# Block products in sevens: two more pairs of strips per layer in a two-layer decoder trunk

## The chip, the cores and the metric

The kernel runs on one core of one Trainium2 chip. The metric is the time of one execution on the device in microseconds (us), as the median of several runs; lower is better. Per core there are a matrix engine (PE in the profile, TensorE), a vector engine (DVE), a scalar engine (ACT), GpSimd (POOL) and the queue that issues most loads (SP). The engines run side by side and wait for one another through semaphores; each takes its own instructions in a fixed order.

## The reference, cut to what matters

A trunk of two layers over 256 tokens with 2048 features. Each layer is attention, then a gated feed-forward part with a short convolution, then a gate with an embedding; everything is residual, in float32.

```python
for i in range(DEPTH):                       # DEPTH = 2
    h = rms_norm(x, attn_norm_w[i])
    x = x + mixer_a(h, ...)                  # layer 0; mixer_b(...) over shared keys and values in layer 1
    x = x + conv_ffn(rms_norm(x, ffn_norm_w[i]), ffn_w_up[i], ffn_conv_w[i], ffn_conv_b[i], ffn_w_down[i])
    gate = jax.nn.sigmoid(rms_norm(x, ple_norm_w[i]) @ ple_w_gate[i])
    x = x + gate * (p[i] @ ple_w_proj[i])

def conv_ffn(h, w_up, conv_w, conv_b, w_down):   # h @ w_up: 256 x 2048 by 2048 x 11264
    u = causal_depthwise_conv(h @ w_up, conv_w, conv_b)
    gate, val = u[..., :D_FF], u[..., D_FF:]     # D_FF = 5632
    return (jax.nn.silu(gate) * val) @ w_down    # 256 x 5632 by 5632 x 2048
```

The attention parts end in an output projection (`wo_a`, 2048 x 2048; `wo_b`, 1536 x 2048), whose result is added to `x` and normed: that is the input `h` of the up projection.

## The kernel before

**Words.** A *block* is 128 input features; an activation block (`h`, `g`, `o`) holds them for all 256 tokens, as a high and a low part, which together carry float32. A *strip* is 512 output columns of a weight matrix; its result is two PSUM banks, one for each 128 tokens (*token half*). For one block, one strip and one token half `add_block` (L339) issues three matmuls of 128x512: L342 (low activation, high weights), L343 (high, low) and L344 (high, high). A *tile* is two blocks of weights of one strip, so 12 matmuls.

**Weights.** `weights` (L277) loads four blocks of a strip at once (`raw`, 1 MB, SP queue, L288; four such buffers). ACT makes the high part of a tile (`whi`, L305) and DVE the low part (`wlo`, L306). The pool `wsp` has four pairs of `whi`/`wlo` (`NWSP`, L70): a pair is free again when PE has read it. So in the steady state ACT and DVE work three to four tiles ahead of PE, and wait for PE to free a pair.

**Seven for eight.** `Seven` (L437) takes four blocks of two strips. Two token halves, two pairs of blocks and two strips would be eight products of two blocks (six matmuls each). It makes seven: `block_sums` (L413) adds and subtracts quarters of the activations once (DVE L423 to L428, split by ACT L431 and DVE L432); `load` (L476) brings both strips' four blocks; `first` to `seventh` each split one weight combination (`parts`, L460, ACT L464 and DVE L465) and multiply (L474), and DVE adds weights in between (L458). `fourth` ends with four additions on PSUM (L514 to L517), which prepare the four result banks. `first` to `fourth` are put among the tiles of the strip before (the *host* strip), at the places in `HEADS`, and `fifth` to `seventh` among those of the pair's own first strip, at `TAILS`; the pair then goes on from its fifth block. The weight combinations are written over the loaded `raw` tiles, which stay taken until the seventh product.

**Where sevens are.** Of 11 pairs of up strips (gate and value) per layer, five go in sevens; of the down projection, which comes in two parts (blocks 0 to 19 after five pairs of up strips, blocks 20 to 43 after the other six), strips 2 and 3 of each part.

**The order around the change.** `add_strips` (L903) makes a projection whose result is added to `x` (L917, DVE), squared for the norm (L211, ACT), and turned from tokens to features: DVE transposes (L243), POOL sends the result to DRAM and fetches it back (L246, L254), and `split_x` (L143 ACT, L144 DVE) makes four blocks `h` of it. The turned strip is used one strip later (`Turned.add`); the last strip's four blocks come late, by `products` (L359), which begins the next matrix with the blocks that are there. For `wo_b` three strips (0, 1, 2) are begun with eight blocks and then get their last four, and strip 3 follows with all twelve; for `wo_a` two strips are begun so.

**The scheduler.** The program's text is not the order on the engines: a scheduler places instructions by priority and its own estimate of times; the weight splits have a higher priority (`AHEAD`) than the `block_sums`.

Of the kernel before, what the change touches and what calls it, by code (L numbers as in the profile page):

```python
# [50 lines left out]
HEADS, TAILS = {8: (1, 3, 5, 7), 6: (1, 2, 4, 5)}, (0, 1, 3)  # L51
# [24 lines left out]
def tile_trunk(ctx, tc, head_d, xT_d, x_d, pT_d, pos_d, vec_d, cst_d, csb_d, wqkv, wo_a, wkv, wq_b, wo_b, wup, wdn, wpg, wpp, gfin_d, out_d):  # L76
# [244 lines left out]
    def strip_v(W, s, xs, base=0, tail=2, ringed=0, begun=None, ends=True, before=lambda k0: None, room=None, halved=False, ready=None, hooks={}):  # L321
# [8 lines left out]
        for k, o, hi, lo in (g for group in it for g in group):  # L330
            if ps[o] is None:
                ps[o] = bank("accv", "acc") if room is None else room[:, o]
                if halved and o:
                    ps[o] = ps[o][:, :S]
            c = slice((o - 1) * S, o * S) if halved and o else slice(0, 512)
            add_block(ps[o], xs[k], min(o, 1), hi[:, c], lo[:, c], k == 0 and not begun, ends and k == n - 1)
# [22 lines left out]
    def products(jobs, xs, late=None, at=0, then={}, side=2, seven=None):  # L359
# [7 lines left out]
        if late is not None:  # L367
            n = len(xs)

# [4 lines left out]
            def before(k0):  # L374
                if k0 == at:
# [4 lines left out]
            hooks = {}  # L380
            if seven is not None:
                tiles = n // 2
                hooks = {tiles - 4: seven.load, tiles - 2: seven.first, tiles - 1: seven.second}
            begun = [
                strip_v(
                    W,
                    s,
                    xs[:n],
                    base,
                    ends=False,  # L390
                    before=before if i == side - 1 else lambda k0: None,
                    room=two_banks() if i == 2 else None,
                    hooks=hooks if i == side - 1 else {},
                )
                for i, (W, s, base) in enumerate(jobs[:side])
            ]
# [5 lines left out]
            hooks = [{0: seven.third}, {0: seven.fourth}] if seven is not None else [{}] * side  # L402
            for b, (W, s, base), more in zip(begun, jobs, hooks):
                yield strip_v(W, s, xs[n:], base + n, begun=b, ready=ready, hooks=more)
                ready = None
            jobs = jobs[side:]
        if seven is not None:
            yield from seven.both()
            jobs = []
        for W, s, base in jobs:  # L410
            yield strip_v(W, s, xs, base)
# [25 lines left out]
    class Seven:  # L437
# [4 lines left out]
        def __init__(self, W, s0, s1, xs, sums, base=0, two=True):  # L442
            self.W, self.strips, self.base, self.two = W, (s0, s1), base, two
# [5 lines left out]
        def value_bank(self, o):  # L449
            if not self.two:  # L450
                return bank("values", "acc")
            if o == 0:
                self.banks = two_banks()
            return self.banks[:, o]
# [29 lines left out]
        def first(self):  # L484
            self.c11 = bank("gates")
# [10 lines left out]
        def second(self):  # L496
            self.c12 = self.value_bank(0)
# [6 lines left out]
        def third(self):  # L504
            self.c21 = bank("gates", "acc")
            self.product(self.c21, self.sums[1], self.parts(self.u), True)

        def fourth(self):
            self.c22 = self.value_bank(1)
# [20 lines left out]

        def go_on(self):
            hooks = dict(zip(TAILS, (self.fifth, self.sixth, self.seventh)))
            yield strip_among(self.W, self.strips[0], self.xs, hooks, [self.c11, self.c21], 4, self.base)

        def end(self, hooks):
            return strip_among(self.W, self.strips[1], self.xs, hooks, [self.c12, self.c22], 4, self.base)

        def both(self):
            yield from self.go_on()
            yield self.end({})  # L540
# [173 lines left out]
    def mixer_a(xs, rc, first):  # L714
# [4 lines left out]

        def turned(which, g, ps=None):  # L720
            us = scaled(ps or strip_v(wqkv, 4 * which + g, xs), (rq, rc)[which], ring_room)
# [500 lines left out]
```

## Time and profile before

| what | value |
|---|---|
| three runs | 2280.32, 2280.76, 2280.83 us; median 2280.76 us |
| the profiled execution: its own time, its span | 2284.18 us, 2282.4 us |
| mean granted PE clock | 0.998 |
| busy: PE, DVE, ACT, POOL | 2267.6, 1686.4, 1318.8, 327.7 us |
| moved by DMA | 538.44 MB, 236 GB/s |

Busy time of PE counts overlapping matmuls once; each matmul's row lasts longer than the distance to the next start. A row "A ... <-B" in the lists reads: result, inputs, count, busy time, mean of one in ns, and the idle time before it with what ended it.

### The profile page before, as it was taken

To read this page: it belongs to the slowest core of one execution; us is meant where nothing else is said; L and a number is where in the kernel's file an instruction comes from. 1 tells how busy PE (TensorE), PEld (TensorE's weight loads), DVE (VectorE), ACT (ScalarE), POOL (GpSimd) and SP (SyncE) were. 2 spreads that over 40 slices of the span, in tenths; PEclk is the share of its full clock that TensorE was granted. 3 is DMA by queue.
4 is the path that set the end of the run, shared out by engine and by line. 5 is a ranking of instruction groups with operands and counts; after the bars stand their busy time and mean duration, and the time that the engine had idled before them with its cause. 6 is when DMAs were issued, how large, how long until landed. Compare 5 with 4: busy or idle time off the path is not lost.

```text
span 2282.4 us, 28059 instructions
## 1 busy us (share of the span) xinstructions
PE 2267.6 (99%) x10113; PEld 1878.2 (82%) x10113; DVE 1686.4 (74%) x2471; ACT 1318.8 (58%) x1766; POOL 327.7 (14%) x575
## 2 busy tenths in 40 slices
PE   9999999999999999999999999999999999999998
PEld 7888888888888888888888888888888888888887
DVE  7656667688875888876667665768887588887665
ACT  6554555666644666655565554666664466665554
POOL 0211111111100111101111331211110011110100
PEclk9999999999999999999999999999999999999999
DMA  8777767676755767758676786767675576775863
GB/s 307 251 240 240 237 224 254 216 271 230 252 199 196 262 232 242 264 185 272 207 266 236 254 261 225 259 217 266 228 252 202 195 256 234 238 265 187 273 222 120
DMA packets 98348, 538.44 MB, mean 236 GB/s; under 512 B 16672, under 2 KB 17568, under 8 KB 46752
## 3 DMA queue, kind: packets, MB, share of 16 engines
q1 hardware_dynamic: 63360, 435.46, 54.6%
q0 software_dynamic: 32560, 95.98, 13.8%
q10 hardware_dynamic: 2288, 5.21, 0.6%
q8 instruction: 79, 1.29, 0.2%
q14 instruction: 61, 0.50, 0.1%
HBM read 486.52 MB, written 50.07 MB: 235 GB/s over the span
## 4 chain that ended last, share of the span: by engine, by line
PE 97%; DMA 2%; ACT 0%; POOL 0%; DVE 0%; issue 0%; POOLq 0%
PE accv L343 22%; PE accv L342 22%; PE accv L344 22%; PE two L343 4%; PE two L344 4%; PE two L342 4%; PE gates L343 4%; PE gates L344 4%; PE gates L342 4%; PE gates L474 3%; PE two L474 3%; PE two L583 1%; DMA turned<-there 1%; DMA there<-y 1%; PE keys L583 0%; POOL turned L254 0%
## 5 line engine op out<-in xcount | busy, mean ns | idle before, releaser
L306 DVE TENSOR_TENSOR wlo<-raw,whi 128x1024 fp32r<-128x1024 f32 (+1 forms) x768 | 931.5, 1215 | 455.2 <-ACT whi L305 452.7
L305 ACT ACTIVATE whi<-raw 128x1024 fp32r<-128x1024 f32 (+1 forms) x768 | 807.6, 1053 | 699.0 <-PE accv L344 426.1
L342 PE MATMUL accv<-whi,h 128*128 128x512 f32 (+1 forms) x1688 | 655.2, 388 | 2.4 <-DVE h L144 2.4
L344 PE MATMUL accv<-whi,h 128*128 128x512 f32 (+1 forms) x1688 | 656.3, 389 | 0.0
L343 PE MATMUL accv<-wlo,h 128*128 128x512 f32 (+1 forms) x1688 | 655.6, 388 | 0.0
L342 PEld LDWEIGHTS accv<-whi,h 128*128 128x128 f32 x1688 | 316.9, 188 | 68.6 <-DVE h L144 1.9
L343 PEld LDWEIGHTS accv<-wlo,h 128*128 128x128 f32 x1688 | 317.0, 188 | 65.8 <-DVE wlo L306 0.7
L344 PEld LDWEIGHTS accv<-whi,h 128*128 128x128 f32 x1688 | 317.0, 188 | 64.6
L246 POOL DMA_DIRECT2D there<-y x162 | 91.5, 565 | 1249.4 <-DVE y L243 1229.9
L254 POOL DMA_DIRECT2D turned<-there x324 | 189.5, 592 | 471.8 <-DMA there<-y 208.7
L464 ACT ACTIVATE whi<-raw 128x1024 fp32r<-128x1024 f32 x98 | 103.7, 1058 | 80.8 <-PE accv L344 68.2
L465 DVE TENSOR_TENSOR wlo<-raw,whi 128x1024 fp32r<-128x1024 f32 x98 | 119.8, 1222 | 34.8 <-ACT whi L464 34.5
L342 PE MATMUL accv<-whi,g 128*128 128x512 f32 x352 | 136.9, 389 | 0.0
L343 PE MATMUL accv<-wlo,g 128*128 128x512 f32 x352 | 136.9, 389 | 0.0
L344 PE MATMUL accv<-whi,g 128*128 128x512 f32 x352 | 136.9, 389 | 0.0
L342 PE MATMUL gates<-whi,h 128*128 128x512 f32 x240 | 93.4, 389 | 0.0
L343 PE MATMUL gates<-wlo,h 128*128 128x512 f32 x240 | 93.4, 389 | 0.0
L344 PE MATMUL gates<-whi,h 128*128 128x512 f32 x240 | 93.4, 389 | 0.0
L342 PE MATMUL two<-whi,h 128*128 128x512 f32 x240 | 93.4, 389 | 0.0
L343 PE MATMUL two<-wlo,h 128*128 128x512 f32 x240 | 93.4, 389 | 0.0
L344 PE MATMUL two<-whi,h 128*128 128x512 f32 x240 | 93.4, 389 | 0.0
L243 DVE STREAM_TRANSPOSE y<-u 128x512 f32<-128x512 f32 x122 | 84.1, 700 | 1.8 <-DMA there<-y 1.3
(224 smaller groups left out, 3024.2 us busy)
## 6 DMA issues: line engine op xcount, KB each, us to landing
raw<-in_wup SPq DMA_DIRECT2D x176, 1024.0 KB, 5.6
raw<-in_wdn SPq DMA_DIRECT2D x88, 1024.0 KB, 5.3
there<-y POOLq DMA_DIRECT2D x171, 256.0 KB, 5.2
turned<-there POOLq DMA_DIRECT2D x324, 128.0 KB, 5.1
raw<-in_wqkv SPq DMA_DIRECT2D x40, 1024.0 KB, 6.6
raw<-in_wpg SPq DMA_DIRECT2D x32, 1024.0 KB, 5.0
raw<-in_wkv SPq DMA_DIRECT2D x24, 1024.0 KB, 5.2
raw<-in_wo_a SPq DMA_DIRECT2D x16, 1024.0 KB, 5.4
```

The costliest lines, as they stand in the source:

```text
L243: last["turned"] = nc.vector.transpose(y.rearrange("p (b o r) -> p o b r", b=4, o=4), strip.rearrange("p (o b c) -> p o b c", o=4, b=4)).ins
L246: nc.gpsimd.dma_start(there[t * P : (t + 1) * P], y)
L254: nc.gpsimd.dma_start(z[32 * b : 32 * b + 32].rearrange("p a o r -> p a (o r)"), back[b])
L305: last["high"] = nc.scalar.activation(hi[:, c], r, AF.Copy).ins
L306: last["low weights"] = nc.vector.tensor_tensor(lo[:, c], r, f32(hi[:, c]), op=OP.subtract).ins
L342: nc.tensor.matmul(ps, xl, hi, start=first, stop=False, skip_group_check=again)
L343: nc.tensor.matmul(ps, xh, lo, start=False, stop=False, skip_group_check=again)
L344: nc.tensor.matmul(ps, xh, hi, start=False, stop=final, skip_group_check=again)
L464: last["high"] = nc.scalar.activation(hi, r, AF.Copy).ins
L465: last["low weights"] = nc.vector.tensor_tensor(lo, r, f32(hi), op=OP.subtract).ins
L474: nc.tensor.matmul(ps, x, y, start=begins, stop=ends, skip_group_check=True)
L583: run.append(nc.tensor.matmul(*args, skip_group_check=True, **kw).ins)
```

## The change

Four sevens more: in each layer the first pair of up strips (gate strip 0, value strip 11), hosted by strip 3 of the output projection (`wo_a`, `wo_b`), and strips 0 and 1 of the second part of the down projection, hosted by the last up strip. `Seven` gets its banks by a list of tags (`take`); `products` begins a pair from a `Seven` that already has four blocks (`first`, `skip = 4`), with `fifth` to `seventh` among the tiles of its first strip; `end` can host the next seven among its six tiles. The sums of blocks 0 to 3 are made once, earlier than before, and shared (`began.sums`, `first.sums`). Parts of the diff under `if False` build nothing and are left out.

```diff
-HEADS, TAILS = {8: (1, 3, 5, 7), 6: (1, 2, 4, 5)}, (0, 1, 3)
+HEADS, TAILS = {10: (2, 4, 6, 8), 8: (1, 3, 5, 7), 6: (1, 2, 4, 5)}, (0, 1, 3)
+PLAN = {-4: "load", -2: "first", -1: "second"}, {0: "third"}, {0: "fourth"}
...
@@ products
+            skip = 4 if first else 0
...
+            if first:
+                hooks[0] = first.rest()
+                begun[:2] = first.banks()
+            if seven:
+                hooks[side - 1].update({(n - skip) // 2 + i: getattr(seven, f) for i, f in plan[0].items()})
+                later = [{i: getattr(seven, f) for i, f in p.items()} for p in plan[1:]]
+            for i, (W, s, base) in enumerate(jobs[:side]):
+                begun[i] = strip_v(
                     W,
                     s,
-                    xs[:n],
-                    base,
+                    xs[skip:n],
+                    base + skip,
                     ends=False,
+                    begun=begun[i],
...
-        for W, s, base in jobs:
-            yield strip_v(W, s, xs, base)
+        for i, (W, s, base) in enumerate(jobs):
+            after = host() if i == len(jobs) - 1 else None
+            yield strip_v(W, s, xs, base, hooks=after.begin(len(xs) // 2) if after else {})
@@ class Seven
+        def rest(self):
+            return dict(zip(TAILS, (self.fifth, self.sixth, self.seventh)))
+
+        def banks(self):
+            return [self.c11, self.c21], [self.c12, self.c22]
...
+        def end(self, after=None):
+            hooks = after.begin(len(self.xs) // 2 - 2) if after else {}
+            return strip_among(self.W, self.strips[1], self.xs, hooks, self.banks()[1], 4, self.base)
@@ ffn
-            sums = block_sums(xs)
+            sums = began.sums if began and late is not None else block_sums(xs)
...
+                    if final and hosts:
+                        after = down[0] = Seven(wdn[i], 0, 1, gs, block_sums(gs[:4]), 4 * strips[0], ("att", "acc", "acc", "acc"))
...
-                        yield from products([(W, s, 0), (W, v, 0)], xs, late, None)
+                        yield from products([(W, s, 0), (W, v, 0)], xs, late, None, first=began)
...
-                        yield from now.go_on()
-                        yield now.end(after.begin(6) if after else {})
+                        yield now.go_on()
+                        yield now.end(after)
...
+            if first:
+                seven = Seven(wdn[i], 2, 3, gs, first.sums, base, ("acc", "two", "acc", "two"))
@@ main loop
-        h, late = add_strips(wo_a if i == 0 else wo_b, o, G_FFN + i * KB, norm, late=o_late, at=(8, 4)[i], side=2 + i)
+        host = lambda h: Seven(wup[i], 0, FB // 4, h, block_sums(h[:4]), 0, ("att", "acc", "acc", "acc"))
+        h, late, began = add_strips(
...
-        h, late, norm = ffn(i, h, late, rc)
+        h, late, norm = ffn(i, h, late, rc, began)
```

**The order on the engines.** In all PE has 24 matmuls fewer (9930 rows for 9954), ACT 20 rows more (12 `whi`, 8 copies), DVE 44 more (12 `wlo`, 16 additions of weights, 16 on PSUM); POOL and SP have as many as before. Line numbers of the changed file are three to ten higher: L308 there is L305 here, L345 to L347 are L342 to L344, L474 is L464, L484 is L474, L146 is L143, L441 is L431, L161 is L158. Numbers behind a name only tell buffers apart.

First place, second layer, ACT, from the fifth tile of strip 3 of `wo_b` on; before (`whi_2272` and `whi_2274` are the fifth and sixth tile, `whi_2301` is the first tile of the up projection):

```order
L305 ACTIVATE whi_2272_12039<-raw_2271_12037 128x1024
L143 ACTIVATE h_2236_11879<-turned_2228_11834,vec_75 128x256
L143 ACTIVATE h_2237_11882<-turned_2228_11834,vec_75 128x256
L143 ACTIVATE h_2238_11885<-turned_2228_11834,vec_75 128x256
L143 ACTIVATE h_2239_11888<-turned_2228_11834,vec_75 128x256
L305 ACTIVATE whi_2274_12055<-raw_2271_12037 128x1024
L158 ACT_TABLE_LOAD
L305 ACTIVATE whi_2301_12146<-raw_2300_12144 128x1024
L305 ACTIVATE whi_2305_12164<-raw_2300_12144 128x1024
```

and in the changed kernel (`whi_2306` and `whi_2311` are the fifth and sixth tile of strip 3, `whi_2309` is the fourth product's weights, `whi_2329` the fifth product's, `sum_2275` and `sum_2279` the two halves of the sums, `h_2265` to `h_2268` the turned strip 1):

```order
L308 ACTIVATE whi_2306_12140<-raw_2305_12138 128x1024
L474 ACTIVATE whi_2309_12157<-raw_2281_12025 128x1024
L146 ACTIVATE h_2265_11977<-turned_2257_11932,vec_75 128x256
L146 ACTIVATE h_2266_11980<-turned_2257_11932,vec_75 128x256
L146 ACTIVATE h_2267_11983<-turned_2257_11932,vec_75 128x256
L146 ACTIVATE h_2268_11986<-turned_2257_11932,vec_75 128x256
L308 ACTIVATE whi_2311_12172<-raw_2305_12138 128x1024
L161 ACT_TABLE_LOAD
L441 ACTIVATE sum_2275_12009<-u_2274_12002 128x512
L474 ACTIVATE whi_2329_12237<-raw_2281_12025 128x1024
L441 ACTIVATE sum_2279_12021<-u_2278_12014 128x512
L308 ACTIVATE whi_2332_12249<-raw_2331_12247 128x1024
```

The turned strips are split later relative to the tiles, and the two sums now stand on ACT between the last tile of strip 3 and the first ones of the up projection.

PE at the end of strip 3 there; before, the up projection's first tile follows at once:

```order
L343 MATMUL accv_2263_11980<-wlo_2275_12056,o_2215_11754 128x512
L344 MATMUL accv_2263_11980<-whi_2274_12055,o_2215_11754 128x512
L342 MATMUL accv_2303_12150<-whi_2301_12146,h_2236_11879 128x512
L343 MATMUL accv_2303_12150<-wlo_2302_12147,h_2236_11879 128x512
L344 MATMUL accv_2303_12150<-whi_2301_12146,h_2236_11879 128x512
```

and in the changed kernel (`seven_2288`, `2294`, `2302` and `2308` are the result banks c11, c12, c21 and c22; weights 2295, 2303, 2309 and 2329 are those of the second, third, fourth and fifth product):

```order
L347 MATMUL accv_2287_12042<-whi_2311_12172,o_2229_11788 128x512
L484 MATMUL seven_2288_12049<-whi_2329_12237,h_2252_11919 128x512
L484 MATMUL seven_2294_12080<-whi_2295_12081,sum_2276_12010 128x512
L484 MATMUL seven_2294_12080<-wlo_2296_12082,sum_2275_12009 128x512
L484 MATMUL seven_2294_12080<-whi_2295_12081,sum_2275_12009 128x512
L484 MATMUL seven_2302_12127<-whi_2303_12128,sum_2276_12010 128x512
L484 MATMUL seven_2302_12127<-wlo_2304_12129,sum_2275_12009 128x512
L484 MATMUL seven_2302_12127<-whi_2303_12128,sum_2275_12009 128x512
L484 MATMUL seven_2308_12156<-whi_2309_12157,sum_2276_12010 128x512
L484 MATMUL seven_2308_12156<-wlo_2310_12158,sum_2275_12009 128x512
L484 MATMUL seven_2308_12156<-whi_2309_12157,sum_2275_12009 128x512
L484 MATMUL seven_2288_12049<-wlo_2330_12238,h_2252_11919 128x512
```

The second, third and fourth product, which the text puts among strip 3's tiles, stand behind its last tile, since their sums come late there.

Second place, first layer, PE, in the fourth tile (2996) of strip 3 of `wo_a`, in the changed kernel (before, only the rows on `accv` stand there); `sum_537` and `sum_541` are the low halves of the two sums:

```order
L484 MATMUL seven_558_2983<-whi_559_2984,sum_537_2895 128x512
L484 MATMUL seven_558_2983<-wlo_560_2985,sum_536_2894 128x512
L484 MATMUL seven_558_2983<-whi_559_2984,sum_536_2894 128x512
L346 MATMUL accv_548_2927<-wlo_562_2997,o_292_1587 128x512
L347 MATMUL accv_548_2927<-whi_561_2996,o_292_1587 128x512
L345 MATMUL accv_548_2927<-whi_561_2996,o_293_1590 128x512
L346 MATMUL accv_548_2927<-wlo_562_2997,o_293_1590 128x512
L484 MATMUL seven_558_2983<-whi_559_2984,sum_541_2907 128x512
```

Here the second product runs inside strip 3, one tile later than an evenly placed one would.

More of the change, by code (lines that the diff above doesn't have):

```diff
@@ L319, in steps, with strip_v @@
             yield [(k0 + i, o, hi[i], lo[i]) for k0, hi, lo in held for i in range(2)]
-    def strip_v(W, s, xs, base=0, tail=2, ringed=0, begun=None, ends=True, before=lambda k0: None, room=None, halved=False, ready=None, hooks={}):
+    def strip_v(W, s, xs, base=0, tail=2, ringed=0, begun=None, ends=True, before=lambda k0: None, room=None, halved=False, ready=None, hooks={}, again=False):
         n = len(xs)
@@ L335, in strip_v @@
             c = slice((o - 1) * S, o * S) if halved and o else slice(0, 512)
-            add_block(ps[o], xs[k], min(o, 1), hi[:, c], lo[:, c], k == 0 and not begun, ends and k == n - 1)
+            add_block(ps[o], xs[k], min(o, 1), hi[:, c], lo[:, c], k == 0 and not begun, ends and k == n - 1, again)
         return ps
@@ L357, in two_strips, with products @@
         return out
-    def products(jobs, xs, late=None, at=0, then={}, side=2, seven=None):
+    def products(jobs, xs, late=None, at=0, then={}, side=2, first=None, seven=None, plan=PLAN, host=lambda: None):
         jobs = list(jobs)
@@ L401, in products @@
                 add()
-            hooks = [{0: seven.third}, {0: seven.fourth}] if seven is not None else [{}] * side
-            for b, (W, s, base), more in zip(begun, jobs, hooks):
-                yield strip_v(W, s, xs[n:], base + n, begun=b, ready=ready, hooks=more)
+            for b, (W, s, base), more in zip(begun, jobs, later):
+                yield strip_v(W, s, xs[n:], base + n, begun=b, ready=ready, hooks=more, again=bool(first))
                 ready = None
             jobs = jobs[side:]
-        if seven is not None:
-            yield from seven.both()
-            jobs = []
-        for W, s, base in jobs:
-            yield strip_v(W, s, xs, base)
+        if seven:
+            yield seven.go_on()
+            yield seven.end(host())
+            return
+        for i, (W, s, base) in enumerate(jobs):
+            after = host() if i == len(jobs) - 1 else None
+            yield strip_v(W, s, xs, base, hooks=after.begin(len(xs) // 2) if after else {})
     def block_sums(xs):
@@ L718, in mixer_a @@
         q, k, ws, os = {}, {}, {}, []
+        sums = block_sums(xs[:4]) if False else None
+        pair = [None]
         def turned(which, g, ps=None):
+            if ps is None and pair[0]:
+                ps = pair[0].end() if which else pair[0].go_on()
             us = scaled(ps or strip_v(wqkv, 4 * which + g, xs), (rq, rc)[which], ring_room)
@@ L901, in mixer_b, with add_strips @@
         return os, lambda: use(z)
-    def add_strips(W, xs, gain_of, norm, base=0, late=None, at=6, side=2):
+    def add_strips(W, xs, gain_of, norm, base=0, late=None, at=6, side=2, first=None, seven=None, plan=PLAN, host=None):
         out = []
@@ L911, in add_strips, with hosted @@
         turned = Turned(use)
-        seven = Seven(W, 2, 3, xs, block_sums(xs[:4]), base) if gain_of is None or base else None
-        for s, ps in enumerate(products([(W, s, base) for s in range(4)], xs, late, at, side=side, seven=seven)):
+        begun = [None]
+        def hosted():
+            if host is not None:
+                begun[0] = host(out)
+            return begun[0]
+        jobs = [(W, s, base) for s in range(4)]
+        for s, ps in enumerate(products(jobs, xs, late, at, {}, side, first, seven, plan, hosted)):
             if norm is not None and s == 3:
@@ L1051, in ple @@
                 gf.append(t)
-        gates = products([(wpg[i], s, 0) for s in range(3 if gain_of is None else 4)], xs, late, None)
+        seven = None
+        if False and gain_of is not None:
+            seven = Seven(wpg[i], 2, 3, xs, block_sums(xs[:4]), 0, ("att", "acc", "acc", "acc"))
+        jobs = [(wpg[i], s, 0) for s in range(3 if gain_of is None else 4)]
+        gates = products(jobs, xs, late, None, seven=seven, plan=PLAN_GATE)
         for s in range(4):
```

96 lines of the change are left out of this document (55 added, 41 removed).

## The prediction

> **What bounds the kernel now.** I read the busy shares and the chain of the page first, then the list of PE's waits, then windows over single stretches. The page's rows:
>
> ```profile
> PE 2267.6 (99%) x10113; PEld 1878.2 (82%) x10113; DVE 1686.4 (74%) x2471; ACT 1318.8 (58%) x1766; POOL 327.7 (14%) x575
> ...
> PE 97%; DMA 2%; ACT 0%; POOL 0%; DVE 0%; issue 0%; POOLq 0%
> ```
>
> PE is busy 99% of the span and carries 97% of the chain that ended last. The list of its waits is short:
>
> ```profile
> PE accv L342 <- DVE h L144: 2.4, 2, 1.4
> PE two L583 <- DMA turned<-there: 1.3, 1, 1.3
> PE warm L125 <- DVE zero L122: 1.2, 1, 1.2
> ```
>
> So time is the number of matmuls, at PE's own pace, and a change pays only by taking matmuls away without making PE wait. The pace is not the 389 ns that a row lasts. In these windows (span, then busy time and instructions of PE, PEld, DVE, ACT, POOL, then granted clock, DMA share, GB/s) the first is a strip that hosts an existing seven: eight tiles and four products, 120 matmuls.
>
> ```profile
> core 0: us, PE busy (x) PEld busy (x) DVE busy (x) ACT busy (x) POOL busy (x), PEclk, DMA share, GB/s
> 894.40:921.57 27.17, 27.17 (x121) 22.50 (x120) 24.86 (x35) 17.95 (x24) 3.47 (x6) 1.00 0.57 194
> 1446.88:1463.20 16.32, 16.32 (x74) 13.52 (x72) 14.54 (x29) 12.52 (x20) 5.33 (x10) 1.00 0.93 304
> ```
>
> 27.17/120 = 0.2264 us from one matmul to the next; the second window, strip 3 of `wo_b`, is 72 matmuls in 16.32, so 0.2267. I take 0.2266: a tile of 12 is 2.72 us, a product of six 1.36. The first window also shows that a seven can be hosted with PE busy throughout, though DVE works 24.86 of 27.17 us. The second shows what is different where the change puts its new one: DVE is at 89% and DMA at 0.93 without any seven.
>
> **What the change takes away.** Each seven has six matmuls fewer; the order shows 9930 rows for 9954. 24 x 0.2266 = 5.44 us, all on the path. By the Trainium skill, page "TensorE: Matmul & The Clock Gate", section "Back-to-back issue gap", matmuls of 512 columns follow at about 131 ns in a stream; by that figure the 24 would be an estimated 3.1 us; the trace shows 226.6 ns, so the measurement decides.
>
> **What it adds.** The prices, from the groups by form (busy, mean ns of one, idle before):
>
> ```profile
> L306 DVE TENSOR_TENSOR wlo<-raw,whi 128x1024 fp32r<-128x1024 f32 x760 | 926.2, 1221 | 454.8 <-ACT whi L305 452.4
> L458 DVE TENSOR_TENSOR raw<-raw 128x1024 f32<-128x1024 f32 x28 | 34.3, 1225 | 0.9
> L514 DVE TENSOR_TENSOR part<-two,part 128x512 f32<-128x512 f32 x14 | 9.6, 684 | 0.0
> L515 DVE TENSOR_TENSOR gates<-gates,part 128x512 f32<-128x512 f32 x14 | 9.7, 692 | 0.0
> L423 DVE TENSOR_TENSOR u<-h 128x256 f32<-128x256 f32 x16 | 6.4, 418 | 0.0
> L432 DVE TENSOR_TENSOR sum<-u,sum 128x512 fp32r<-128x512 f32 x16 | 11.0, 687 | 1.4 <-ACT sum L431 1.4
> L144 DVE SCALAR_TENSOR_TENSOR h<-turned,vec,h 128x256 fp32r<-128x256 f32 x80 | 34.6, 478 | 17.9 <-ACT h L143 17.8
> L305 ACT ACTIVATE whi<-raw 128x1024 fp32r<-128x1024 f32 x760 | 803.0, 1058 | 698.6 <-PE accv L344 426.1 <-PE two L344 110.6 <-PE gates L344 79.7
> L158 ACT ACT_TABLE_LOAD x8 | 10.3, 1283 | 0.9 <-PEq L1210 0.7
> ```
>
> A seven adds three `whi` (3.2 us of ACT) and two copies there (at most L432's 0.69 each), three `wlo`, four additions of weights and four on PSUM (3.67 + 4.9 + 2.75 = 11.3 us of DVE). Spread over a host of 16 us and the strip after, that is hidden as long as no pair of `wsp` is blocked. Loads are the same 1 MB pieces from the same matrices in another order; POOL and SP issue as many as before, and I cost their order at nothing: the `raw` tiles are asked for a strip ahead. What costs is where PE's next row needs something that has just begun.
>
> *Second layer, up pair, hosted by strip 3 of `wo_b`.* Strip 3 begins at V0 = 1447.0 (first row). The sums need the turned strip 0, whose `y` (second row) gives `h` (third row) 12.4 us later:
>
> ```profile
> 1447.08 1.29 DVE L917 TENSOR_TENSOR x<-two,x 128x512 f32<-128x512 f32 x2 [0.40 <-PE two L344]
> 1438.64 0.70 DVE L243 STREAM_TRANSPOSE y<-x 128x512 f32<-128x512 f32 x1
> 1451.77 1.71 ACT L143 ACTIVATE h<-turned,vec 128x256 fp32r<-128x256 f32 x4 [0.91 <-DMA turned<-there]
> ```
>
> That is V0 + 4.8, in time for the first product (about V0 + 6.4). But DVE splits weights before it makes sums, and then splits the turned strip 1, which lands at V0 + 12.1 and so right among them:
>
> ```profile
> 1459.10 0.91 ACT L143 ACTIVATE h<-turned,vec 128x256 fp32r<-128x256 f32 x2
> ```
>
> So the order puts both sums, and with them the second to fourth product, behind strip 3's last tile. These three products hold three of the four `wsp` pairs (2295, 2303, 2309) while they wait, and one pair must serve tile 2306, then 2311, then the fifth product's 2329. At each turn PE stops until the pair is filled again:
> - tile 2311: `whi` 1.06 and `wlo` 1.22, less the two matmuls (0.45) that need only the high part: at least 1.83; 2.2 with strip 1's four splits (4 x 0.5) partly between them.
> - 2329: at least one `whi`, 1.06, its `wlo` being needed only ten rows later. The table load (1.28) and `sum_2275` stand ahead on ACT: I take 1.35.
> - Strip 0's own tile on c21 (`seven_2302`), seven rows or 1.59 us after the fourth product ends: DVE has L514 (0.68), a `wlo` (1.22) and L515 (0.69), 2.59, ahead of it: 1.0 late; I take 1.1.
> - 0.35 for `wlo_2299` at the first tiles and 0.4 for small ones.
>
> Sum 2.2 + 1.35 + 1.1 + 0.75 = 5.4. The low end leaves only the first two floors, 2.9; the high end, 7.0, adds a whole table load to 2329 (1.28) and one more `wlo` part (0.35) at 2311.
>
> *What the later strips get.* Before, PE loses time at the turned strip 2, whose `y` to `h` takes 18.3 us and which it waits for:
>
> ```profile
> 1455.64 0.70 DVE L243 STREAM_TRANSPOSE y<-x 128x512 f32<-128x512 f32 x1
> ...
> 1473.85 0.39 PE L344 MATMUL accv<-whi,h 128*128 128x512 f32 x1
> 1474.60 0.51 ACT L143 ACTIVATE h<-turned,vec 128x256 fp32r<-128x256 f32 x1 [4.38 <-DMA turned<-there]
> 1475.68 0.50 PE L342 MATMUL accv<-whi,h 128*128 128x512 f32 x1 [1.45 <-DVE h L144]
> ```
>
> Between the two PE rows lie 1.83 us, so 1.6 are lost. In the changed order PE reaches these blocks some 6 us later (two strips' first four blocks come by seven products, and the pauses above stand ahead). The `y` is made at the same place, so this pause goes: -1.6. If the transfer slips as well, it is 0.
>
> *First layer, up pair, hosted by strip 3 of `wo_a`.* Here the sums do come inside the host. Strip 3 begins with these x additions (T0 = 356.87):
>
> ```profile
> 356.89 1.28 DVE L917 TENSOR_TENSOR x<-accv,x 128x512 f32<-128x512 f32 x2
> 378.65 1.28 DVE L917 TENSOR_TENSOR x<-accv,x 128x512 f32<-128x512 f32 x2
> 381.58 0.70 DVE L243 STREAM_TRANSPOSE y<-x 128x512 f32<-128x512 f32 x1
> 388.41 2.34 POOL L254 DMA_DIRECT2D turned<-there  x4 [5.28 <-DMA there<-y]
> ...
> turned<-there POOLq DMA_DIRECT2D x324, 128.0 KB, 5.1
> ```
>
> From there to `sum_541` DVE has the two additions (1.3), six of `wlo` or weight additions (7.3), two `y` (1.4), four splits of `h` (1.9) and two sums (1.4): 13.3 with nothing else between, some 0.4 less as the first two lie in part ahead; PE asks for it 56 rows in, 12.7. I take 0.2. The second risk is the last turned strip. Its `y` is ready 3.6 us after strip 3's end before (382.28 - 378.65). In the changed order four rows on PSUM (2.75), three `wlo` (3.66) and the four splits of strip 2 (1.9) come ahead of it: 8.3 more, so it is ready about 12.0 after. From `y` to landing the rows show 13.0 (388.41 + 2.34, less the last issue's own time, + 5.1 - 382.28), and 1.0 for the first split: 26.0; PE arrives after 114 rows, 25.8. So 0.2 to 0.4, and up to 2 if that transfer is as slow as the 18.3 above in part. Term: 0.6 (0.2 to 2.0).
>
> *Down sevens, both layers.* The host is the last up strip, six tiles and 16.3 us; its blocks `g` lie there long before. The order has the second product's sum ready 6.9 to 8.1 us after the host's start on DVE, and PE asks for it at 7.5: 0 to 0.65 each; I take 0.3 each, 0.6 together.
>
> **The sum.** -5.44 - 1.6 + 5.4 + 0.6 + 0.6 = -0.44. The profiled execution took 2284.18 us, 3.4 over the median of the runs; all terms are differences, so I put them to the median: 2280.76 - 0.44 = 2280.3. The lowest of the forecast's own case is -5.44 - 1.6 + 2.9 + 0.2 = -3.9, so 2276.8; the highest -5.44 + 7.0 + 2.0 + 1.3 = +4.9, so 2285.6. That both ends straddle no change is the point: a gain of 5.4 us on PE, and about as much given back by one host that has no room.
>
> **Rivals.**
> *All four are hidden, as the existing ones are.* For it speaks the window at 894: DVE 24.86 of 27.17 us and no pause. Against it the window at 1447, where DVE has 14.54 of 16.32 us taken already, and the pairs counted above. It gives 2280.76 - 5.44 = 2275.3, with the pause at strip 2 gone 2273.7. Chance 0.13.
>
> *Slower: the turned strip 0 of `wo_b` comes as late as strip 2.* The new hosting asks for `h` of strip 0 about V0 + 6.4, for the first product; before, nothing needed it until strip 3 was over. If its way takes 18.3 in place of 12.4 us (the new loads of 2 MB fall into a stretch with DMA at 0.93), its split is done at V0 + 10.8: 4.4 us of waiting inside the host. It decides from 14 us on. With the strip 2 pause kept (+1.6), 2280.3 + 4.4 + 1.6 = 2286.3. Chance 0.07.
>
> *Slower: the clock.* The mean granted clock of the run is below one:
>
> ```profile
> core 0: 2282.4 us, clock 0.998
> ...
> 0.00:10.00 10.00, 7.80 (x25) 3.95 (x26) 3.92 (x7) 4.50 (x7) 0.20 (x4) 1.00 0.81 251
> 1475.70:1479.10 3.40, 3.40 (x15) 2.82 (x16) 2.97 (x8) 2.52 (x5) 2.34 (x4) 1.00 0.76 268
> ```
>
> 0.2% of 2282.4 is 4.6 us; if the row of short pauses in each up host cost that once more, 2280.3 + 9.1 = 2289.4. Against it: the first ten us have 2.2 us without PE and are granted 1.00, and so is the stretch right behind the 1.83 us pause. The Trainium skill, same page, section "A second HAM failure mode: psum-queue depth-cycling", says that frequent short idle times between groups of matmuls can make the clock gate swing between half and full rate; no row here shows it. Chance 0.03.
>
> That the change does nothing is no case: the order has the 24 matmuls fewer.
>
> **How the numbers follow.** The forecast has 0.77. No change is within 0.2%, about what a measurement of this kernel can tell apart: 2276.2 to 2285.3. The forecast's own range lies in it but for its last 0.3. Faster is the first rival, 0.13; slower the other two, 0.10; same 0.77. The forecast's own range holds a little less than 8 in 10, so the low end goes to the nearer value of the first rival: 2275.3 to 2285.6.
>
> **What would show it.** Right: 9930 matmuls at the same 0.2266; PE's list of waits names, in strip 3 of `wo_b` and just behind it, a wait for `whi` (L308) or `wlo` at the sixth tile and at the fifth product, together 3 to 4 us, and one on `seven` for L525 near 1; the wait of 1.4 for `h` of strip 2 is gone; in `wo_a` and the down hosts only pauses below 0.7. Wrong: none of the waits in `wo_b` (then the first rival, and the pairs were filled in time), a wait for `turned` at the first product (the second), a granted clock below 1.00 in a window around the up hosts (the third), or DVE pauses of over 1 us in the down hosts, which I cost at 0.3 each.

## The result, and the profile after

The changed kernel takes 2297.82 us (median of 6 runs, 2294.13 to 2300.67), the kernel before 2281.11 (6 runs): 16.7 us more, a ratio of 1.0072 (95% interval 1.0062 to 1.0082; the ratios here and below are worked out over all the runs, so they are not the exact quotient of the medians). The forecast was 2280.3, and its range ended at 2285.6. The changed kernel's page has:

```profile
PE 2270.5 (99%) x10089; PEld 1875.2 (82%) x10089; DVE 1723.5 (75%) x2515; ACT 1333.3 (58%) x1786; POOL 328.8 (14%) x575
...
PE 91%; DMA 3%; DVE 3%; issue 2%; ACT 1%; POOL 0%; SPq 0%; DVEq 0%; ACTq 0%; POOLq 0%
```

PE has its 24 matmuls fewer (10089 rows for 10113) and is still "99% busy", but it carries 91% of the chain, not 97%: other engines and DMA are now on the path. Its list of waits has become long:

```profile
PE accv L345 <- ACT whi L308: 3.7, 1, 3.7
PE seven L484 <- DVE sum L442: 3.6, 2, 1.8
PE seven L345 <- DVE seven L526: 1.9, 1, 1.9
PE two L346 <- DVE wlo L309: 1.5, 2, 0.8
PE seven L484 <- ACT whi L474: 1.2, 1, 1.2
...
PE seven L345 <- DVE h L147: 0.7, 1, 0.7
...
PE two L345 <- ACT whi L308: 0.4, 1, 0.4
```

These waits do not hold all of it. For the whole I added up, over all starts of PE but those of its warm-up, the distance to the next start less 0.2266 us. It gives about 25.7 us lost after and 7.4 before, so 18.3 more; less the 5.44 of the matmuls that is 12.9, and the two spans differ by 13.1 (2295.5 and 2282.4). By place, lost before and after:

| place | before | after |
|---|---|---|
| strip 3 of `wo_b` and the strips behind it (1440 to 1500 us) | 1.8 | 11.4 |
| down host, first layer (940 to 960) | 0 | 3.9 |
| down host, second layer (2020 to 2060) | 0 | 5.1 |
| strip 3 of `wo_a` and the strip behind it (360 to 420) | 0 | 1.6 |
| all the rest | 5.6 | 3.7 |

The profiled execution of before took 2284.18 us, 3.1 over the median of its six runs, and has a 1.4 us wait at 77 us which the one of after lacks; that is where the 13.1 here and the 16.7 of the medians part.

**The largest pause.** In strip 3 of `wo_b`, PE, then ACT (start, duration, engine, line):

```profile
1463.47 0.39 PE L347 MATMUL accv<-whi,o 128*128 128x512 f32 x1
1467.51 1.22 PE L345 MATMUL accv<-whi,o 128*128 128x512 f32 x2 [3.65 <-ACT whi L308]
1468.77 0.80 PE L346 MATMUL accv<-wlo,o 128*128 128x512 f32 x1
1469.37 0.63 PE L347 MATMUL accv<-whi,o 128*128 128x512 f32 x1
```

```profile
1461.18 1.06 ACT L474 ACTIVATE whi<-raw 128x1024 fp32r<-128x1024 f32 x1 [1.66 <-DVE u L433]
1464.81 1.70 ACT L146 ACTIVATE h<-turned,vec 128x256 fp32r<-128x256 f32 x4 [2.57 <-DMA turned<-there]
1466.42 1.04 ACT L308 ACTIVATE whi<-raw 128x1024 fp32r<-128x1024 f32 x1
```

ACT waits 2.57 us for the turned strip 1, splits it for 1.7, and only then makes the last tile's high part, for which PE has waited since 1463.7. The four splits stand ahead of it in ACT's order, and nobody needs them yet.

**The clock.** Behind this pause the matmuls follow at 0.42 to 0.43 us, not 0.23 (1469.37 to 1469.79 is one step). In windows over this place, and over the second layer's down host (the clock is third from the end):

```profile
1465.00:1470.00 5.00, 2.45 (x5) 1.54 (x6) 4.13 (x7) 3.74 (x6) 2.35 (x4) 0.64 0.43 118
1470.00:1475.00 5.00, 3.80 (x10) 2.48 (x10) 2.97 (x9) 1.69 (x2) 0.00 (x0) 0.68 0.54 201
1475.00:1480.00 5.00, 5.00 (x24) 4.12 (x23) 3.95 (x7) 2.27 (x4) 1.13 (x2) 1.00 0.17 66
2048.00:2054.00 6.00, 5.45 (x17) 4.33 (x18) 6.00 (x9) 3.21 (x6) 1.13 (x2) 0.72 0.56 161
```

For some us behind the pauses about half the clock is granted. The slow steps (0.28 to 0.6 us) cost 2.1 and 1.7 us more than 0.2266 each would, so 3.8 of the 18.3.

**The down hosts.** In the first layer, SP, ACT, DVE and PE:

```profile
923.39 4.19 SPq L490 DMA_DIRECT2D raw<-in_wdn  x2
928.38 5.64 SPq L291 DMA_DIRECT2D raw<-in_wup  x2
...
raw<-in_wup SPq DMA_DIRECT2D x1, 1024.0 KB, 11.6
```

```profile
940.13 1.06 ACT L308 ACTIVATE whi<-raw 128x1024 fp32r<-128x1024 f32 x1 [4.74 <-DMA raw<-in_wup]
951.12 0.68 DVE L442 TENSOR_TENSOR sum<-u,sum 128x512 fp32r<-128x512 f32 x1
951.86 0.50 PE L484 MATMUL seven<-whi,sum 128*128 128x512 f32 x1 [1.79 <-DVE sum L442]
```

The new seven's two loads (L490) go out at 923.4 and 927.2, ahead of the host's own first one. That one goes out at 928.4, when DVE's last reading of a buffer ends (a `wlo`, 927.14 to 928.36), and lands 11.6 us later (last row of the first list), at 940.0; the median of these loads in this run is 5.4. So it is late twice: it has to wait for a buffer, and then takes twice as long as usual, with a load that went out 1.1 us before it still under way. ACT has been idle for 4.74 us by then. Everything in the host is late, and DVE's sum as well: PE waits once at the first tile and once for the sum.

### The profile page after: what moved, and what is told of

Its sections match the earlier page's. It is cut to its first block, busy times and chain, and to the rows that moved or that the text cites. A ratio compares the mean times of both kernels' runs of the same rounds, so it can differ in the third digit from the quotient of the medians.

```text
span 2295.5 us, 28075 instructions
## 1 busy us (share of the span) xinstructions
PE 2270.5 (99%) x10089; PEld 1875.2 (82%) x10089; DVE 1723.5 (75%) x2515; ACT 1333.3 (58%) x1786; POOL 328.8 (14%) x575
## 4 chain that ended last, share of the span: by engine, by line
PE 91%; DMA 3%; DVE 3%; issue 2%; ACT 1%; POOL 0%; SPq 0%; DVEq 0%; ACTq 0%; POOLq 0%
PE accv L346 18%; PE accv L347 18%; PE accv L345 18%; PE seven L345 6%; PE seven L347 6%; PE seven L346 6%; PE seven L484 4%; PE two L345 4%; PE two L346 4%; PE two L347 4%; PE two L484 2%; PE two L595 1%; DMA raw<-in_wup 1%; DVE wlo L309 1%; DMA turned<-there 1%
## 5 line engine op out<-in xcount | busy, mean ns | idle before, releaser
L308 ACT ACTIVATE whi<-raw 128x1024 fp32r<-128x1024 f32 (+1 forms) x752 | 790.2, 1053 | 674.6 <-PE accv L347 356.8
L347 PE MATMUL accv<-whi,h 128*128 128x512 f32 (+1 forms) x1560 | 606.5, 389 | 0.0
L346 PE MATMUL accv<-wlo,h 128*128 128x512 f32 (+1 forms) x1560 | 605.7, 388 | 0.2 <-DVE wlo L309 0.2
L345 PE MATMUL accv<-whi,h 128*128 128x512 f32 (+1 forms) x1560 | 605.3, 388 | 0.5 <-DVE h L147 0.5
L345 PEld LDWEIGHTS accv<-whi,h 128*128 128x128 f32 x1560 | 292.9, 188 | 61.4 <-ACT whi L308 1.7
L346 PEld LDWEIGHTS accv<-wlo,h 128*128 128x128 f32 x1560 | 292.9, 188 | 61.0 <-DVE wlo L309 0.8
L347 PEld LDWEIGHTS accv<-whi,h 128*128 128x128 f32 x1560 | 292.9, 188 | 59.9
L474 ACT ACTIVATE whi<-raw 128x1024 fp32r<-128x1024 f32 x126 | 133.2, 1058 | 101.0 <-PE accv L347 60.9
L475 DVE TENSOR_TENSOR wlo<-raw,whi 128x1024 fp32r<-128x1024 f32 x126 | 153.7, 1220 | 37.0 <-ACT whi L474 36.4
L345 PE MATMUL seven<-whi,h 128*128 128x512 f32 x336 | 130.9, 390 | 2.6 <-DVE seven L526 1.9
L346 PE MATMUL seven<-wlo,h 128*128 128x512 f32 x336 | 130.8, 389 | 0.2 <-DVE wlo L309 0.2
L347 PE MATMUL seven<-whi,h 128*128 128x512 f32 x336 | 130.7, 389 | 0.0
L345 PE MATMUL seven<-whi,g 128*128 128x512 f32 x304 | 118.4, 389 | 0.0
L347 PE MATMUL seven<-whi,g 128*128 128x512 f32 x304 | 118.3, 389 | 0.0
L346 PE MATMUL seven<-wlo,g 128*128 128x512 f32 x304 | 118.3, 389 | 0.0
L345 PE MATMUL two<-whi,h 128*128 128x512 f32 x240 | 94.3, 393 | 0.5 <-ACT whi L308 0.4
L347 PE MATMUL two<-whi,h 128*128 128x512 f32 x240 | 93.9, 391 | 0.0
```

What stands on the lines that cost most here:

```text
L308: last["high"] = nc.scalar.activation(hi[:, c], r, AF.Copy).ins
L345: nc.tensor.matmul(ps, xl, hi, start=first, stop=False, skip_group_check=again)
L346: nc.tensor.matmul(ps, xh, lo, start=False, stop=False, skip_group_check=again)
L347: nc.tensor.matmul(ps, xh, hi, start=False, stop=final, skip_group_check=again)
L474: last["high"] = nc.scalar.activation(hi, r, AF.Copy).ins
L475: last["low weights"] = nc.vector.tensor_tensor(lo, r, f32(hi), op=OP.subtract).ins
```

## The experiments

All times stand beside runs of the kernel before on the same chip. Theories: **Q**, in `wo_b` ACT's order puts waiting splits ahead of needed weights; **P**, the prediction's, three held pairs of `wsp` leave one; **R**, in the down hosts two sevens back to back hold the raw buffers; **K**, pauses lower the clock.

### One part alone: which place costs what

First `host if i in (0,)` and no down sevens (e1), then `i in (1,)` (e2), then the down sevens alone (e3).

```diff
-            host=host if True else None,
+            host=host if i in (0,) else None,
...
-        gs, late, silu, first = part(range(half, FB // 4), hosts=True)
+        gs, late, silu, first = part(range(half, FB // 4), hosts=False)
```

> Only the first layer's up seven (hosted by strip 3 of wo_a); the other three are undone. Six matmuls fewer, 1.36 us. If the four places add up, as the trace after suggests, it keeps the pauses seen there (0.5 in the host, 0.9 at the last turned strip) and comes out even: 2281 us. If the loss after is one of all four together (the clock lower for the whole run), it is a clean gain of 1.4: 2279.7.

> Only the second layer's up seven (hosted by strip 3 of wo_b). Theory Q (on ACT the splits of the turned strip 1 stand ahead of the last tile's high part and wait for the transfer; 3.8 us at that tile, then half clock for some 5 us): -1.4 - 1.6 + 11.4, so about 2289.5, with one PE wait of over 3 us for L308. Rival P, the prediction's (only pairs of wsp are short, each pause about one high and one low part): -1.4 - 1.6 + 5.4, 2283.5, no wait over 2.3.

> Only the two down sevens (hosts: the last up strip of each layer), twelve matmuls fewer, 2.7 us. If they cost by themselves what the trace after shows (1.6 at the host's first tile, 1.95 at the second product's sums, twice, and 1.7 of clock): -2.7 + 8.9, so 2287, or 2285.5 without the clock. Rival: the pauses come from the shifted up part; then the prediction's 0.6 holds, 2279.

Measured, beside 2282.70: e1 2286.79 (ratio 1.0021, 1.0011 to 1.0032), e2 2293.97 (1.0060, 1.0047 to 1.0073), e3 2289.66 (1.0034, 1.0022 to 1.0046). Each place loses by itself, so the loss is not that of all four together, and not of a shifted up part. Added up they are 1.15%, not 0.72%: the same waits come in other sizes. The list of e2, then of e1, then of e3:

```profile
PE accv L345 <- ACT whi L308: 5.4, 1, 5.4
```

```profile
PE seven L345 <- DVE h L147: 1.9, 1, 1.9
```

```profile
PE seven L484 <- DVE sum L442: 3.6, 2, 1.8
...
PE two L345 <- ACT whi L308: 1.6, 2, 0.9
PE two L346 <- DVE wlo L309: 1.5, 2, 0.8
```

e2 has theory Q's wait, far over P's 2.3. At 5.4 it is larger than the 3.7 of the change, but the profiled execution of e2 was its slowest (2303.15 us, with a 2.2 us wait elsewhere), so the size is that of this execution. e3 has the down hosts' waits as in the change. e1 was a miss: I expected 2281, and it is 4 over before. The wait for the last turned strip is 1.9 there (0.7 in the change) with 1.7 us of slow steps behind it.

### The down hosts

e4 gives five raw buffers, with a smaller ring of activation blocks to make room (`NRING, NRAW = 38, 5`). e6 keeps four, moves the loads one tile later, products to tiles 3 to 6, and gives the sums priority:

```diff
-... 6: (1, 2, 4, 5)}, (0, 1, 3)
+... 6: (3, 4, 5, 6)}, (0, 1, 3)
...
-            return {0: self.load, ...
+            return {int(tiles == 6): self.load, ...
...
+                        with tc.high_priority(offset=AHEAD):
+                            early = block_sums(gs[:4])
```

> The two down sevens with five raw buffers for four (the ring of activation blocks 38 for 42, to make room). Theory R (two sevens back to back hold four raw buffers, so the host's first load is issued late): the wait for L308/L309 at the host's first tile, 1.6 in each layer, goes, and the wait for the sums, 1.95 each, stays: 3.2 us faster than with four buffers. Rival: the load is late since DMA is busy; then the first wait stays and the time is that of four buffers.

> The two down sevens with two edits: their two loads are issued one tile later, behind the host's first own load, and products among tiles 3 to 6; and the sums have the priority of the weight splits. Theory R: both the wait at the host's first tile and that for the sums go, and with them the lower clock: 2.7 us under the kernel before, where the sevens as they are were 7.0 over it. Rival: with two sevens back to back four buffers are too few wherever the loads stand; then a wait of 1 to 2 us for L308 or L309 comes two tiles later, and the time is 1 to 5 over.

e4: 2288.62, 1.0026 (1.0015 to 1.0037); e6: 2282.41 beside 2282.66, 0.9999 (0.9990 to 1.0007). PE's waits in e4, then in e6:

```profile
PE seven L346 <- DVE wlo L309: 3.0, 5, 0.8
PE seven L484 <- DVE sum L442: 1.9, 2, 1.0
```

```profile
PE seven L346 <- DVE wlo L309: 1.7, 2, 1.0
```

With a fifth buffer the wait at the host's first tile is gone, so R holds for it, though the rival, a busy DMA, has a share in how late the load was: the host's first load goes out only 1.4 us earlier (929.3; 930.7 in e3), but the load ahead of it is 3.9 us ahead, not 1.1, and it lands in 6.6 us, not 12.2. The wait for the sums shrinks to 0.9 and 1.0, since the host is in time, but stays. Waits of 3.0 for low parts come elsewhere; whether the smaller ring or the fifth buffer brings them was not separated (e13 below has the smaller ring and none of them, but no down sevens either). So the time hardly falls (expected 3.2, measured 1.0 with overlapping intervals). With both mends of e6 neither wait is left, nor a slow clock; 1.7 us come in the strips behind. The loss of 7 is gone, the gain of 2.7 isn't there to see.

### The last turned strip

e7 is e1 with the last strip's addition to `x` and its transposes at the priority of the weight splits.

```diff
+                with tc.high_priority(offset=AHEAD) if host is not None and s == 3 else ExitStack():
                     last["added"] = nc.vector.tensor_tensor(...)
...
+            with tc.high_priority(offset=AHEAD) if self.soon and s == 3 else ExitStack():
                 self.strip = (s, turn(s))
```

> The first layer's up seven alone, with the addition to x and the transposes of the last strip of wo_a given the priority of the weight splits, so that they stand ahead of the seven's additions on DVE. If the 2.1 us wait for the last turned strip, and the 1.7 of lower clock behind it, come from the late transpose (12 us after the strip's end, 3.6 without the seven), both go: 1 under the kernel before, 4 to 5 less than without the edit. Rival: the transfer itself takes longer, since DMA is busy; then the wait stays over 1.

2283.29 beside 2282.66, 1.0002 (0.9993 to 1.0011), 3.5 under e1. The wait is gone, and the clock is 1.00 there. The host's window in e7:

```profile
356.00:384.00 28.00, 27.89 (x122) 22.55 (x122) 23.25 (x27) 18.63 (x25) 3.48 (x6) 1.00 0.55 188
```

DVE is busy 23.25 of 28.0 us: it fits, though the gain expected, 1 us, is below what can be told.

### The host in `wo_b`

e5 is e2 with the splits of strip 1 behind strip 3's last high part; e9 adds e7's edit; e13 adds to e9 a fifth pair (`NRING, NWSP = 38, 5`); e14 instead gives the sums priority.

```diff
+        def split(self):                        # called at strip 3's end
+            with tc.issue_after(last["high"]):
+                self.use(*held)
...
+            if self.hold and s == 2:
+                self.held = self.strip
```

> The second layer's up seven alone, with the splits of the turned strip 1 put on ACT behind the high part of strip 3's last tile. Theory Q: the wait of 5.4 us for L308 at that tile goes, and with it the lower clock behind it, at least 7 us faster than the same seven without this (11.3 over the kernel before), so at most 4.5 over it. Rival P (pairs of wsp are short): a wait of about 2 us stays at that tile, and the gain is 3 to 4 us.

> The second layer's up seven alone, splits of strip 1 late as in the run before, and the last strip's addition and transposes of wo_b with priority as in the first layer's mended run. If the 4.0 us wait for the last turned strip and the 2.8 of lower clock behind it come from the late transpose, both go: 7 less, 1 to 2 over the kernel before, with the pauses that shared pairs of wsp give (1.3 and 0.8 at the last tile, 0.6 at the fifth product, 2.0 at c21) left. Rival: the transfer on a busy DMA takes that long anyway; then over 3 us stay.

> As e9 (second layer's up seven alone, both mends), with five pairs of weights for four and the ring of activation blocks 38 for 42. The prediction's step (three held pairs leave one): the waits of 1.15 and 0.53 at strip 3's last tile and 0.4 at the fifth product go, those at c21 stay: 2.5 to 3 less than e9's 7.0 over the kernel before, or 5 if the lower clock goes too. If pairs are not it, the waits stay.

> As e9, with the sums given the priority of the weight splits, four pairs. In the order the second to fourth product then begin inside strip 3, two rows' worth ahead of its last tile. If the late sums are the root (they hold the pairs and push c21's additions against the up projection), waits at the last tile and at c21 shrink to under 1 in all and the time is that of the kernel before or 1 to 2 under it. If the sums then hold up DVE's weight splits, new waits for L320 of the same size come in strip 3 and it stays 3 or more over.

| run | median, before beside it | ratio |
|---|---|---|
| e5 | 2292.48, 2282.66 | 1.0038 (1.0025 to 1.0052) |
| e9 | 2289.68, 2282.71 | 1.0035 (1.0022 to 1.0048) |
| e13 | 2290.44, 2281.49 | 1.0039 (1.0026 to 1.0051) |
| e14 | 2289.50, 2281.49 | 1.0036 (1.0023 to 1.0050) |

The expected times were at most 4.5 over the kernel before for e5, 1 to 2 for e9, 2 to 4.5 for e13, and for e14 at most 0 or, on its rival, 3 or more. Measured are 9.8, 7.0, 9.0 and 8.0: three misses and e14's rival, though each edit shrinks the wait that it was made for. The lists of e5, e9, e13 and e14 show why (in e9's first row, 1.1 of the 2.3 is at the program's start):

```profile
PE seven L354 <- DVE h L147: 4.0, 1, 4.0
PE seven L354 <- DVE seven L535: 1.8, 1, 1.8
```

```profile
PE accv L356 <- ACT whi L319: 2.3, 2, 1.1
PE seven L356 <- DVE seven L537: 1.2, 1, 1.2
...
PE seven L495 <- DVE wlo L486: 0.9, 1, 0.9
PE accv L357 <- DVE wlo L320: 0.9, 2, 0.5
```

```profile
PE seven L495 <- DVE sum L453: 4.9, 1, 4.9
PE seven L495 <- DVE seven L538: 1.5, 1, 1.5
```

```profile
PE seven L495 <- DVE wlo L486: 2.4, 1, 2.4
PE seven L356 <- DVE seven L537: 1.5, 1, 1.5
```

In e5 Q's wait falls from 5.4 to 1.1, so ACT's order was its cause; but a wait of 4.0 for the last turned strip takes its place. In e9 that one is gone, as expected, and what P foretold is left, 2.1 us at the last tile and more at c21. In e13, with five pairs, the waits for pairs are gone, and one of 4.9 for the sums stands there: P's pairs were not the root either. In e14 the sums are early, and PE waits for low parts. What is common to them is DVE. From 1450 to 1480 us it is busy 29.17 of 30 us in e5, 29.09 in e9 and 28.80 in e14. In e13:

```profile
1450.00:1460.00 10.00, 10.00 (x46) 8.24 (x45) 9.79 (x16) 7.83 (x14) 4.04 (x7) 1.00 0.72 236
1460.00:1470.00 10.00, 6.43 (x29) 4.96 (x27) 10.00 (x18) 4.10 (x5) 3.51 (x6) 1.00 0.72 224
```

DVE works 9.79 and 10.00 of each 10 us there while PE falls to 6.43. From 1446.1 to 1473.6 it is never idle for more than 0.3 us. Before, strip 3 of `wo_b` had 14.54 of 16.32 us of DVE; the seven brings 11.3 more, over a strip lengthened by one or a few products. In all four orders DVE ends late, and the wait moves to what was put last. That DVE is short is read from its rows, not shown by an edit: I did not try one that takes DVE work out of that strip.

### All mended, and three of four

e10 is all four sevens with all mends; e11 leaves `wo_b`'s out.

> All four sevens, with all mends (splits of strip 1 late, last turn soon, down loads one tile later, down sums first). If the terms add up: -5.4 + 0.6 (wo_a) + 4.7 (pairs and c21 in wo_b) - 1.5 (pause at strip 2 gone) + 1.7 (down) = 0 over the kernel before, 15 to 17 under the change as it is. If the four disturb each other, more than 3 over.

> The first layer's up seven and the two down sevens, mended; the second layer's up seven left out. -4.1 + 0.6 + 1.7 = 1.8 under the kernel before, 2281 if that is 2282.7 again; the best of the versions here. Within 0.2% either way, so only the pauses can tell.

e10: 2289.87 beside 2282.71, 1.0033 (1.0020 to 1.0045); e11: 2281.08, 0.9999 (0.9990 to 1.0008). My sum for e10 was 7 too low, and that for e9 5 to 6: it is `wo_b`'s seven that costs. e11 has 18 matmuls fewer (4.1 us), and its longest wait but for the start is 0.5; by the medians it is 1.6 under (expected 1.8), yet it cannot be told from the kernel before. No version here beats it beyond the interval.

### The clock by itself

e8 and e12 are the kernel before with extra copies on ACT, which delay one high part, at ten places far from any seven's sums; the copies are used by nothing.

```diff
+    def pause(n):
+        q = tt("sq", (P, 768), tag="e", bufs=1)[:, :512]
+        ...
+                    stall[0] = nc.scalar.activation(q, strip_of(0, 0), AF.Copy).ins
```

> The kernel before, with 21 to 32 extra copies on ACT (512 columns each, not used) at ten plain pairs of up strips, so that PE waits for a high part there for different lengths. If a pause by itself lowers the clock, windows behind pauses of over about 2 us show a granted clock near 0.5 for a few us, and those behind shorter ones 1.00; if it is what the sevens do, all show 1.00.

> The kernel before with 5 to 14 extra copies on ACT at the same ten places, so that PE waits there between 0 and about 6 us. The longer pauses (8 to 15 us) were each followed by some 4.5 us at half pace. If there is a length below which nothing follows, it shows here: 1.6 (the kernel before) had none, 1.95 had it once in two. If any pause does it, those of 1 us have it too.

e8 (2423.14, one run): ten pauses, 110.2 us in all. A slow stretch follows each of the ten, the first of them in the window here:

```profile
PE accv L343 <- ACT whi L306: 110.2, 10, 14.5
```

```profile
443.00:448.00 5.00, 4.96 (x12) 3.37 (x12) 4.22 (x4) 2.40 (x3) 0.00 (x0) 0.50 0.38 123
```

Behind these pauses of 8 to 15 us, the matmuls at 0.43 us add 0.8 to 2.2 us each. e12 (2298.66, one run) has a wait of 1.6 us or more for a high part at three of the ten places. Each is shown here in time order, then the 3.41 us in which it falls and those behind them; why 3.41 is said below:

```profile
889.37 0.74 PE L343 MATMUL accv<-whi,h 128*128 128x512 f32 x2 [1.61 <-ACT whi L306]
1892.84 0.50 PE L343 MATMUL accv<-whi,h 128*128 128x512 f32 x1 [1.85 <-ACT whi L306]
1983.30 0.50 PE L343 MATMUL accv<-whi,h 128*128 128x512 f32 x1 [2.27 <-ACT whi L306]
```

```profile
886.82:890.23 3.41, 1.68 (x7) 0.73 (x5) 0.88 (x1) 3.35 (x6) 1.64 (x3) 1.00 0.13 38
890.23:893.64 3.41, 3.01 (x7) 2.43 (x8) 3.41 (x4) 1.93 (x3) 0.72 (x2) 0.50 0.58 156
1890.34:1893.75 3.41, 1.38 (x5) 0.49 (x4) 0.93 (x1) 3.38 (x6) 2.35 (x4) 1.00 0.46 131
1893.75:1897.16 3.41, 3.06 (x7) 2.48 (x8) 3.41 (x4) 1.88 (x2) 0.00 (x0) 0.50 0.26 61
1979.08:1982.49 3.41, 1.95 (x9) 1.29 (x7) 0.00 (x0) 3.31 (x6) 2.06 (x4) 1.00 0.20 54
1982.49:1985.91 3.42, 2.08 (x8) 1.43 (x9) 2.63 (x3) 3.42 (x4) 0.29 (x1) 1.00 0.34 104
1985.91:1989.32 3.41, 3.41 (x17) 2.82 (x16) 2.00 (x2) 0.18 (x1) 0.00 (x0) 1.00 0.72 247
```

So K holds without any seven: the pause alone does it. The longest of the three, 2.27, has nothing behind it, the two shorter ones have; and in e3 one layer's down host has it, the other with the same two pauses does not. The traces settle what decides. In each of them the clock changes only at instants that lie whole multiples of 3.413 us apart (in e8 all twenty slow and fast stretches are such multiples); where this grid begins differs from one execution to the next. The windows above are cut on e12's grid, and each comes out at 1.00 or 0.50. The pause of 2.27 lies across a boundary, so PE is busy 1.95 and 2.08 us of the two steps; each of the other two lies in one step, with the beginning of a shorter wait for the low part behind it, and leaves 1.68 and 1.38.

For every step from a trace's first clock record to its last matmul I counted the work: 3.41 us less the time by which the distance from one start of PE to the next is over 0.2266. In the 16 traces 62 steps have 1.39 us of work or less, and each is followed by a step at 0.50; the other 10615 have 1.41 or more, and each is followed by one at 1.00. It holds in both directions, into the slow pace and out of it. The nearest two are one of the changed kernel (2046.66 to 2050.08, 1.39) and one of e5 (1472.45 to 1475.86, 1.41). In e3's second down host the emptiest step has 1.30 and is followed by 0.50; in the first it has 1.63 and is not. This rule is read from the traces above; no run was made to test it.

## Why the prediction was wrong

**What held.** 24 matmuls at 0.2266 us, 5.44. The pause at strip 2 of `wo_b` is gone (1.6). Behind strip 3 of `wo_b`, the wait at the fifth product is 1.2 (1.35 worked out). The arithmetic of the last turned strip in `wo_a`: transposes done 11.9 us behind the strip's end (12.0 worked out), PE there after 25.9 (25.8), and the transfer 13.6 (13.0), so 0.9 and not 0.3.

**The step on `wo_b`, 5.4, measured 11.4 with the clock's share.** Two things in it failed. The tile 2311 was priced at 2.2 "with strip 1's four splits (4 x 0.5) partly between them": their own time, not the wait for the transfer that they carry into ACT's queue. In before the splits of this strip began 12.2 us behind the start of strip 3 (1459.10 and 1446.88), and the last tile was due at 13.6; after, its transfer took longer (why was not tested), they began at 16.5 (1464.81 and 1448.29), and the tile was due at 15.4. It measured 4.6 (3.8 and 0.8 for the low part); e5, where the splits stand behind the tile, shows the cause. The wait on c21, 1.1 in the sum, measured 1.9, and the lower clock, at nothing in the sum, 2.1. The other is the frame: "hidden as long as no pair of `wsp` is blocked". Pairs were counted, and rightly (e9 has 2.1 at that tile); DVE's time was not. 14.54 and 11.3 us against a strip of 16.32 and a product or two stood in the prediction's own rows, and e13 and e14 show that about the same time is lost with pairs enough or sums early. That e9's waits without the clock, 7.1, come near the 5.4 is partly luck: with the pairs' waits taken away (e13), others of the same size stand in their place.

**The step on loads: "I cost their order at nothing: the `raw` tiles are asked for a strip ahead".** True of the sevens that the trace of before shows, whose hosts are plain strips. The down hosts are the first whose own pair is a seven, so all four raw buffers are spoken for, and the host's first load goes out late and lands late (11.6 us). It cost 1.6 at the first tile in the first layer and made the sums late by 1.95 for the 0.3 that I took: the two layers lose 3.9 and 5.1 (1.7 of it the clock) in place of 0.6 in all. e4 shows it, e6 removes it.

**The third rival, 0.03.** It came true in part: 3.8 us. I argued from two rows at clock 1.00, and neither could show it. Behind the pause of 1.83 there is nothing since it left PE busy 1.96 us of its step (1472.44 to 1475.85), which is 1.80 us of work, over the 1.41 that was still enough. Of the first ten us the trace has no record of the clock before 4.7, and the view prints 1.00 there. The Trainium skill, page "TensorE: Matmul & The Clock Gate", section "Why this matters for your kernels", asks for no gaps of PE above about 3 us, at the price of a return to half rate. The trace agrees on the price (0.50 in e8), and not on the length, since pauses of 1.61 and 1.85 had it too: what counts here is how much of one 3.41 us step they take.

**The first rival**, all hidden, is out; **the second**, strip 0 late, did not happen, but the same mechanism struck one strip later, at strip 1, where I did not look for it.

## What to carry to other kernels

When work is put beside a busy engine, add up what each engine does in that stretch, not only what buffers allow: if the sum is over the stretch, removing one wait may only show the next, as four orders did here. An operation that waits for a transfer costs its queue the wait, not its own duration; look at what stands behind it. And count shared buffers for the worst overlap that the new schedule can make, here two sevens back to back, not for those that the old trace shows.

## What was unexpected of the hardware

In these traces PE's clock is set anew in steps of 3.41 us, by the work of the step before: with 1.39 us of matmuls or less the next step is at half pace (0.43 us a matmul for 0.23), with 1.41 or more at full pace, in all 10677 steps of the 16 traces. So it is not the length of one pause that counts: several short ones in a step add up (1.61 and what stood behind it in e12), and one of 2.27 across a boundary is followed by nothing. Where the boundaries fall differs from one execution to the next, so whether a pause of 2 us costs more than itself is luck in any one of them. A pause costs its length and, in e8, up to 2.2 us on top.
